# Gate pairs by seven half-width products, an input cut into blocks, and a second attention moved forward by a conv tile

## The chip, the cores and the metric

One core of a Trainium2 chip runs the whole program. The metric is the time of one execution on the device in microseconds (us); lower is better. The engines go by the profile's names: PE is TensorE (matmuls), PEld its weight loads, DVE is VectorE, ACT is ScalarE, POOL is GpSimd, SP is SyncE, which here issues all DMAs. All five run their own instruction streams in a fixed order and wait for one another by semaphores.

## What is computed

Two layers over a sequence of 512 positions with 1024 channels, batch 1, all in float32. Each layer:

```
h = rms_norm(x, norm_g[l])
p = h @ w_in[l]                          # 1024 -> 8776 columns, split among the mixers and the merge gates
y_a = short_conv_mixer(...)              # 512 wide, width-3 causal conv, gates, then @ w_out_conv (512 -> 1024)
y_b = sparse_attention_mixer(...)        # 8 heads of 64; an indexer picks 128 keys a query; then @ w_out_attn
y_c = pool_mixer(...)                    # causal means over 2, 4, 8, 16 positions; then @ w_out_pool
g = sigmoid(mgate.reshape(B, S, 3, D))   # three gates of 1024 columns each, from p
merged = g[:, :, 0] * y_a + g[:, :, 1] * y_b + g[:, :, 2] * y_c
x = x + merged @ w_o[l]
```

## The kernel before

Everything is held transposed: channels on the 128 partitions, the 512 positions along the free axis. The normalized input is 8 tiles of 128 x 512, and each weight column block of 128 is a chunk of 128 x 1024 (8 k-tiles side by side), streamed from HBM. To keep float32's precision with matmuls of type float32r, every operand is split into a high and a low part: ScalarE copies it to float32r (`hi`), VectorE subtracts that from the source (`lo`), and `mm3` (L393) forms hi*hi + hi*lo + lo*hi, three matmuls for each k-tile.

A projection (`project`, L456) is thus 8 k-tiles x 3 matmuls of 512 columns into one PSUM tile of tag `pj` (four of them). `take` and `prep` (L362 to L381) keep the weights three chunks ahead: a load of 512 KB, ScalarE's copy (L371), VectorE's subtraction (L372). `load_x` (L415) splits the input times `norm_g` into `xh`; the root-mean-square factor `rb` of each position comes later, as a multiplication when a projection leaves PSUM (`evac`, L383).

A layer runs, in program order: the indexer's projections and rotary embedding; four pool tiles, with the selection of keys (`select`, L556; long sequences of VectorE instructions); `merge` for branch C; q and k projections of heads 0 to 3 (`qk_quad`, L679, with norm, rotary embedding and DMAs that stack heads by partitions); v; attention of heads 0 to 3 among the gate projections of the attention (L773); four conv tiles of four projections each (L780), with the second `qk_quad` at tile 3 (L781) and the second `attention` behind them (L803); `merge` for branch A (gates "gA") and branch B ("gB"); and the output projection w_o (L826).

`merge` (L591) takes the 1024 gate columns in four pairs of 128-column tiles. For a pair: two projections of the input (2 x 24 matmuls), evacuated by `rb` and through a tanh (sigmoid(g) is written as (tanh(g/2) + 1)/2), then two output projections `py` of the mixer's 512 channels (2 x 12 matmuls), a product of gate and `py` on VectorE (L608), and a sum into `acc` on POOL (L610). With the last branch the sum is split into `mh`, `ml` for w_o.

The order of work is not that of the program. A planner (`Order`, L30 to L299) reads all instructions, gives each a cost (`cost`, L108) and a latency between engines (L37), plays them through list scheduling (`play`, L139) under the numbers of buffers of every tag, and fixes each engine's order by what came out best in PASSES tries (`arrange`, L247). On PE the priority is program order; what is later fills PE wherever what is earlier isn't ready.

SBUF tags that the change touches: `b` (tiles of 128 x 4 x 512, eight of them), `xhi`/`xlo` (one buffer for each k), `k` (one: the stacked keys of an attention), `ptr` (two: transposed scores), `score1` to `score3`, `h`, `z`, `a`, `w`.

Of the kernel before, what the change touches and what calls it, by code (L numbers as in the profile page):

```python
# [5 lines left out]
F32 = mybir.dt.float32  # L6
F32R = mybir.dt.float32r
# [5 lines left out]
PASSES = 4  # L13
# [16 lines left out]
class Order:  # L30
# [7 lines left out]
    TO_PE = {"PE": 0.003, "DVE": 0.255, "Activation": 0.27, "Pool": 0.2, "SP": 0.27}  # L38
# [37 lines left out]
    def read(self):  # L76
        ops, hist, memo = [], {}, {}
        for inst in self.tc.nc.cur_bb.bb.instructions[self.start:]:
# [6 lines left out]
            for aps, w in ((inst.ins, False), (inst.outs, True)):  # L85
                for a in aps:
                    if hasattr(a, "bass_ap"):
# [4 lines left out]
                        acc.append((w,) + memo[key])  # L92
            for w, name, (p0, p1), mask in acc:
                tiles.append(name)
                h = hist.setdefault(name, [])
                for j, wj, q0, q1, m in h:
                    if (w or wj) and p0 < q1 and q0 < p1 and (isinstance(m, dict) or isinstance(mask, dict) or m & mask):
                        deps.add(j)
# [9 lines left out]
    def cost(self, inst, kind):  # L108
# [14 lines left out]
        if kind == "InstMatmult":  # L123
            f32 = str(aps[0].dtype).endswith("float32")
            c = (0.0004167 * n + 0.003) * ((4 if n > 128 else 2) if f32 else 1)
# [6 lines left out]
        if engine == "Pool":  # L132
            return (0.1 if kind == "InstMemset" else 0.1 + 0.0022 * n), 0.0
        if kind in ("InstMax", "InstMatchReplace"):
            return 0.069 + 0.00104 * max(size(a) for a in aps), 0.0
# [167 lines left out]
def trunk(ctx, tc, xT, wst, vecs, cst, outT):  # L303
# [6 lines left out]
    bp = pool("bp", 8)  # L310
# [46 lines left out]

    wq = {}
# [3 lines left out]
    def prep(i):  # L362
        l, c = divmod(i, NCHUNK)
        raw = wp.tile([P, 1024], F32, tag="raw", name=nm("raw"), bufs=2)
        hi = wp.tile([P, 1024], F32R, tag="whi", name=nm("whi"), bufs=3)
        lo = wp.tile([P, 1024], F32R, tag="wlo", name=nm("wlo"), bufs=3)
        n = 1024 // (4 if i == 0 else 2 if i < 3 else 1)
        for j in range(0, 1024, n):
            p = slice(j, j + n)
            load(raw[:, p], wst[l, c, :, p])  # L370
            act.activation(hi[:, p], raw[:, p], AF.Copy)  # L371
            dve.tensor_tensor(out=lo[:, p], in0=raw[:, p], in1=hi[:, p].bitcast(F32), op=ALU.subtract)  # L372
        wq[i] = (hi, lo)

    def take():
        i = state["used"]
        state["used"] += 1
        while state["next"] <= min(i + LOOK - 1, DEPTH * NCHUNK - 1):
# [36 lines left out]
    def load_x(l, k, xt):  # L415

        g = vt[:, l, V_G + k:V_G + k + 1]
# [57 lines left out]
    for l in range(DEPTH):  # L475
# [115 lines left out]
        def merge(yh, yl, acc, first, last):  # L591
            for d2 in range(0, KT, 2):
                gs = []
                for _ in range(2):
# [6 lines left out]
                for e, g in enumerate(gs):  # L601
                    d = d2 + e
                    py = pj()
# [176 lines left out]
        for i in range(4):  # L780
            if i == 3:  # L781
                quad = qk_quad()
# [161 lines left out]
```

## Time and profile before

| | |
|---|---|
| median of 3 runs | 1079.21 us (1078.87 to 1079.73) |
| the profiled execution | 1078.84 us, of which the span of its instructions is 1077.1 us |
| PE busy | 1065.4 us (99%), 4842 matmuls |
| PEld busy | 878.4 us, 4842 loads |
| DVE busy | 799.2 us (74%), 1389 instructions |
| ACT busy | 465.5 us (43%) |
| POOL busy | 97.2 us (9%) |
| HBM read / written | 101.49 / 4.19 MB, 98 GB/s over the span |
| TensorE's granted clock | 1.00 in every stretch asked for below |

The trace is of one execution, with times in microseconds from the first instruction. The busy time of PE is a union of recorded matmuls, each of which overlaps the next, so the distance from one start to the next start says what a matmul costs in a row. A group of instructions is named by its line in the kernel, its engine, and what it writes and reads (`pj<-xhi,whi`), with buffer numbers left out; nearly all matmuls have line 388, that of the helper `mm`.

### The profile page before, as it was taken

The numbers are of one execution on the slowest core, as the hardware profiler recorded it, in microseconds if no ns is written. First come the engines' busy times: TensorE is split into PE (matmuls) and PEld (weight loads), VectorE is DVE, ScalarE is ACT, GpSimd is POOL, SyncE is SP. The second block draws the span as 40 slices with busy tenths as digits, with TensorE's granted clock in tenths as the row PEclk, the third lists the DMA queues.
The fourth block names the chain that finished last, engine by engine and source line by source line (L and its number), as shares of the span: only waits on it lengthen the run. The fifth ranks groups of instructions, "written<-read, shape, count | busy, mean of one in ns | idle before, by whom it ended". The sixth has DMA issues, their size and how long they took to land.

```text
span 1077.1 us, 13444 instructions
## 1 busy us (share of the span) xinstructions
PE 1065.4 (99%) x4842; PEld 878.4 (82%) x4842; DVE 799.2 (74%) x1389; ACT 465.5 (43%) x747; POOL 97.2 (9%) x76
## 2 busy tenths in 40 slices
PE   7999999999999999999999999999999999999998
PEld 6888888888888888888888888888888878888886
DVE  6889999997558865455559899999876598744442
ACT  6355233485233673233334542235852347623320
POOL 4000000000000011221210000000000001132210
PEclk9999999999999999999999999999999999999999
DMA  6542322452234522234535322225423245122352
GB/s 226 153 140 78 99 98 94 133 152 72 82 102 130 160 75 78 98 98 164 169 117 153 115 86 98 98 79 166 128 79 98 79 144 149 61 98 98 98 195 78
DMA packets 44402, 124.39 MB, mean 115 GB/s; under 512 B 6960, under 2 KB 7472, under 8 KB 44336
## 3 DMA queue, kind: packets, MB, share of 16 engines
q1 hardware_dynamic: 44336, 123.53, 36.4%
q8 instruction: 38, 0.62, 0.2%
q14 instruction: 28, 0.23, 0.1%
HBM read 101.49 MB, written 4.19 MB: 98 GB/s over the span
## 4 chain that ended last, share of the span: by engine, by line
PE 96%; DVE 1%; DMA 1%; issue 0%; ACT 0%; SPq 0%; DVEq 0%; ACTq 0%
PE pj L388 87%; PE sc L388 4%; PE pv L388 3%; PE pt L391 2%; DMA b<-in_x 0%; DVE wlo L372 0%; DMA k<-h 0%; DVE w L488 0%; SPq L355 0%; DVE h L401 0%; ACT whi L371 0%; DVE w L649 0%; ACT xhi L403 0%; DVE w L435 0%; DVE w L436 0%
## 5 line engine op out<-in xcount | busy, mean ns | idle before, releaser
L388 PE MATMUL pj<-xhi,whi 128*128 128x512 f32 x1040 | 373.1, 393 | 6.5 <-ACT whi L371 6.5
L388 PE MATMUL pj<-xlo,whi 128*128 128x512 f32 x1040 | 372.8, 393 | 0.0
L388 PE MATMUL pj<-xhi,wlo 128*128 128x512 f32 x1040 | 372.4, 393 | 0.0
L371 ACT ACTIVATE whi<-raw 128x1024 fp32r<-128x1024 f32 (+2 forms) x185 | 191.5, 1036 | 385.6 <-PE pj L388 358.9
L372 DVE TENSOR_TENSOR wlo<-raw,whi 128x1024 fp32r<-128x1024 f32 (+2 forms) x185 | 228.5, 1239 | 15.5 <-ACT whi L371 14.8
L388 PEld LDWEIGHTS pj<-xhi,whi 128*128 128x128 f32 x1040 | 195.0, 188 | 46.7 <-ACT whi L371 6.7
L388 PEld LDWEIGHTS pj<-xhi,wlo 128*128 128x128 f32 x1040 | 195.7, 188 | 39.4 <-DVE wlo L372 0.5
L388 PEld LDWEIGHTS pj<-xlo,whi 128*128 128x128 f32 x1040 | 195.5, 188 | 39.4
L388 PE MATMUL pj<-b,whi 128*128 128x512 f32 x640 | 210.7, 390 | 0.0
L385 DVE TENSOR_TENSOR w<-pj,ss 128x512 f32<-128x512 f32 x104 | 70.8, 684 | 93.3 <-PE pj L388 93.0
L388 PEld LDWEIGHTS pj<-b,whi 128*128 128x128 f32 x640 | 120.0, 188 | 24.2
L388 PE MATMUL pj<-b,wlo 128*128 128x512 f32 x320 | 118.2, 391 | 0.0
L610 POOL TENSOR_TENSOR b<-b,w 128x512 f32<-128x512 f32 x32 | 60.6, 1899 | 264.5 <-DVE w L608 264.4
L388 PEld LDWEIGHTS pj<-b,wlo 128*128 128x128 f32 x320 | 60.1, 188 | 12.3
L576 DVE MAX8 m<-score 128x8 f32<-128x256 f32 (+2 forms) x96 | 53.2, 557 | 1.7
L577 DVE MATCH_REPLACE8 score<-m,score 128x384 f32<-128x384 f32 (+2 forms) x96 | 52.0, 542 | 0.0
L742 DVE TENSOR_TENSOR pth<-pt,pth 128x128 fp32r<-128x128 f32 (+1 forms) x64 | 31.1, 486 | 18.7 <-PE pv L388 9.4
L819 DVE TENSOR_TENSOR w<-pj,w 128x512 f32<-128x512 f32 x16 | 11.0, 690 | 44.4 <-PE pj L388 42.8
L727 ACT ACTIVATE a<-a,mn 128x128 f32<-128x128 f32 (+1 forms) x64 | 35.6, 557 | 15.5 <-DVE mn L724 14.9
L665 POOL TENSOR_TENSOR w<-w,w 128x512 f32<-128x512 f32 x8 | 11.9, 1492 | 325.4 <-ACT w L664 325.4
L388 PE MATMUL pv<-pth,b 128*128 128x512 f32 (+3 forms) x128 | 39.9, 316 | 0.0
L741 ACT ACTIVATE pth<-pt 128x128 fp32r<-128x128 f32 (+1 forms) x64 | 27.6, 432 | 27.4 <-PE pt L391 20.1
(119 smaller groups left out, 999.7 us busy)
## 6 DMA issues: line engine op xcount, KB each, us to landing
raw<-in_w SPq DMA_DIRECT2D x177, 512.0 KB, 3.3
b<-h SPq DMA_DIRECT2D x128, 64.0 KB, 2.2
k<-h SPq DMA_DIRECT2D x64, 128.0 KB, 3.2
b<-in_x SPq DMA_DIRECT2D x8, 256.0 KB, 4.8
w<-in_x SPq DMA_DIRECT2D x8, 256.0 KB, 5.5
xs<-w SPq DMA_DIRECT2D x8, 256.0 KB, 2.3
w<-xs SPq DMA_DIRECT2D x8, 256.0 KB, 3.9
out_x<-w SPq DMA_DIRECT2D x8, 256.0 KB, 2.0
```

Source lines behind the costliest of these rows:

```text
L371: act.activation(hi[:, p], raw[:, p], AF.Copy)
L372: dve.tensor_tensor(out=lo[:, p], in0=raw[:, p], in1=hi[:, p].bitcast(F32), op=ALU.subtract)
L385: dve.tensor_tensor(out=out, in0=ps, in1=by, op=ALU.mult)
L388: pe.matmul(ps, lhs, rhs, start=start, stop=stop)
L391: pe.transpose(out, src, ident if n == P else ident[64:64 + n, 64:64 + n])
L576: dve.max(m8, score)
L577: dve.match_replace(score, m8, score, -3.0e38)
L610: gp.tensor_tensor(out=a, in0=a, in1=g, op=ALU.add)
L665: gp.tensor_tensor(out=s0, in0=s0, in1=s1, op=ALU.add)
L727: act.activation(pr[:, :w], pr[:, :w], AF.Exp, bias=mn, scale=-1.0, accum_out=zs)
L741: act.activation(dh, pst[:, :b + 1, :], AF.Copy)
L742: dve.tensor_tensor(out=dl, in0=pst[:, :b + 1, :], in1=dh.bitcast(F32), op=ALU.subtract)
```

## The change

Five of the eight gate pairs of branches A and B in each layer (the last pair of "gA", all four of "gB") are computed by Strassen's scheme. The 256 gate columns x 1024 channels of a pair are cut into 2 x 2 blocks (two column tiles by two halves of the channels, four k-tiles each), the input into 2 x 2 blocks (two halves of the channels by two halves of 256 positions). Instead of eight block products there are seven, on sums of blocks. `build` makes the input's blocks once a layer, behind the conv tiles: it loads x again, multiplies by `norm_g` and `rb`, and splits three blocks and four sums into tiles of the tags `b`, `k`, `ptr` and `score`. `prep` makes the sums of weights of each pair from two raw chunks (the layout in HBM has the same number of chunks). `blocks` does the seven products of 12 matmuls of 256 columns, and adds them up on VectorE. The signs are such that one gate's sum comes out negative, hence the `sign` at the tanh.

Besides: the second `qk_quad` goes from conv tile 3 to conv tile 1 and the second attention from behind the conv tiles to conv tile 3; `xh` moves into tiles of tag `b` (twelve instead of eight); `py` of the block pairs uses the PSUM tag `sc`; the planner's costs for matmuls, POOL and one VectorE instruction are changed, its latency from PE to PE becomes 0, PSUM accesses are widened to whole banks when it looks for dependences, and it makes six passes.

```diff
@@ constants, class Order
-PASSES = 4
+QUAD, ATT = 1, 3
+FIRST = 3
+PASSES = 6
-    TO_PE = {"PE": 0.003, "DVE": 0.255, "Activation": 0.27, "Pool": 0.2, "SP": 0.27}
+    TO_PE = {"PE": 0.0, "DVE": 0.255, "Activation": 0.27, "Pool": 0.2, "SP": 0.27}
+        def banks(mask):
+            bank = (1 << S) - 1
+            return (bank if mask & bank else 0) | (bank << S if mask >> S else 0)
...
-            c = (0.0004167 * n + 0.003) * ((4 if n > 128 else 2) if f32 else 1)
+            c = (0.000423 * n + 0.01) * ((4 if n > 128 else 2) if f32 else 1)
...
-            return (0.1 if kind == "InstMemset" else 0.1 + 0.0022 * n), 0.0
+            return (0.1 if kind == "InstMemset" else 0.1 + 0.003 * n), 0.0
...
-    bp = pool("bp", 8)
+    bp = pool("bp", 12)
@@ prep
+        if part == 1:
+            raw = big(F32)
+            c0, c1 = (raw[:, 2 * j:2 * j + 2].rearrange("p a b -> p (a b)") for j in range(2))
+            load(c0, wst[l, c])
+            load(c1, wst[l, c + 1])
+            state["raw"] = c0, c1
+            split(hi, lo, c0)
+            ah, al = (wk.tile([P, S], F32R, tag="a", name=nm("ua"), bufs=4) for _ in range(2))
+            split(ah, al, c1[:, S:])
+            wq[i] += (ah, al)
+            return
+        c0, c1 = state["raw"]
+        a22, a11, a21, a12 = c0[:, :S], c0[:, S:], c1[:, :S], c1[:, S:]
+        u = wk.tile([P, 2, S], F32, tag="h", name=nm("u"), bufs=2)
+        if part == 2:
+            dve.tensor_tensor(out=u[:, 0], in0=a21, in1=a22, op=ALU.add)
+            dve.tensor_tensor(out=u[:, 1], in0=u[:, 0], in1=a11, op=ALU.add)
+            state["s2"] = u[:, 1]
+        else:
+            dve.tensor_tensor(out=u[:, 0], in0=a21, in1=a11, op=ALU.add)
+            dve.tensor_tensor(out=u[:, 1], in0=state["s2"], in1=a12, op=ALU.add)
+        split(hi, lo, u.rearrange("p a b -> p (a b)"))
@@ load_x
-        hi = xp.tile([P, S], F32R, name=nm("xhi"), tag=f"xhi{k}")
-        lo = xp.tile([P, S], F32R, name=nm("xlo"), tag=f"xlo{k}")
-        split(hi, lo, xt, g)
-        xh[k] = (hi, lo)
+        if k % 4 == 0:
+            xh["b"] = big(), big()
+        xh[k] = tuple(b[:, k % 4] for b in xh["b"])
+        split(*xh[k], xt, vt[:, l, V_G + k:V_G + k + 1])
@@ new: build (the loop over k)
+            for k in range(4):
+                x = []
+                for j in range(2):
+                    xj = A() if j else wk.tile([P, S + 16], F32, tag="z", name=nm("z"), bufs=3)[:, :S]
+                    load(xj, xT[k + 4 * j] if l == 0 else xs[k + 4 * j])
+                    g = vt[:, l, V_G + k + 4 * j:V_G + k + 4 * j + 1]
+                    dve.scalar_tensor_tensor(xj, xj, g, rb, op0=ALU.mult, op1=ALU.mult)
+                    x += [xj[:, :q], xj[:, q:]]
+                x11, x12, x21, x22 = x
...
+                split(*t["11", k], x11)
...
+                split(*t["21", k], x21)
...
+                split(*t["22", k], x22)
+                uv = wk.tile([P, 2, S], F32, tag="h", name=nm("uv"), bufs=2)
+                u, v = uv[:, 0], uv[:, 1]
+                dve.tensor_tensor(out=u[:, :q], in0=x11, in1=x12, op=ALU.subtract)
+                dve.tensor_tensor(out=v[:, :q], in0=u[:, :q], in1=x22, op=ALU.add)
+                dve.tensor_tensor(out=u[:, q:], in0=x22, in1=x12, op=ALU.subtract)
+                dve.tensor_tensor(out=v[:, q:], in0=v[:, :q], in1=x21, op=ALU.subtract)
...
@@ new: product and blocks
+        def product(out, part, at, t, name):
+            hi, lo = part
+            for k in range(4):
+                c = slice(at + k * P, at + (k + 1) * P)
+                mm3(out, hi[:, c], lo[:, c], *t[name, k], k == 0, k == 3)
+
+        def blocks(t, a, b):
+            w1, w2, w3 = take(), take(), take()
+            w1, w4 = w1[:2], w1[2:]
...
+            p0, p1, p2, p3 = pj(), pj(), pj(), pj()
+            s, u = W(), W()
...
+            product(p0[:, h0], w1, S, t, "11")
+            act.activation(s[:, h0], p0[:, h0], AF.Copy)
+            product(p2[:, h1], w1, 0, t, "4")
+            product(p3[:, h1], w2, S, t, "2")
+            add(s[:, h1], s[:, h0], p3[:, h1], ALU.subtract)
+            product(p1[:, h0], w2, 0, t, "1")
+            product(p1[:, h1], w3, 0, t, "3")
+            add(pair(u), pair(p1), s[:, h1].unsqueeze(1).to_broadcast([P, 2, q]))
+            add(b[:, h1], p1[:, h0], u[:, h1])
+            add(b[:, h0], p2[:, h1], u[:, h1])
+            product(p2[:, h0], w3, S, t, "22")
+            add(a[:, h1], p2[:, h0], u[:, h0])
+            product(p3[:, h0], w4, 0, t, "21")
+            add(a[:, h0], p3[:, h0], s[:, h0])
@@ merge
+                t = d2 >= 2 * plain
+                if t:
+                    gs = [W(), W()]
+                    blocks(bt, *gs[::-1])
+                    for g, sign in zip(gs, (-1, 1)):
+                        act.activation(g, g, AF.Tanh, scale=0.5 * sign)
...
-                    py = pj()
+                    py = sc() if t else pj()
@@ the layer
-            if i == 3:
+            if i == QUAD:
                 quad = qk_quad()
+            if i == ATT:
+                attention(1, *quad)
...
-        attention(1, *quad)
-        merge(yh, yl, acc, False, None)
+        build()
+        merge(yh, yl, acc, False, None, FIRST)
...
-        merge(yh, yl, acc, False, (mh, ml))
+        merge(yh, yl, acc, False, (mh, ml), 0)
```

## Rows read from the trace of the kernel before

**Rows 1.** the page: busy time of the engines; tenths busy in 40 slices

```profile
PE 1065.4 (99%) x4842; PEld 878.4 (82%) x4842; DVE 799.2 (74%) x1389; ACT 465.5 (43%) x747; POOL 97.2 (9%) x76
...
PE   7999999999999999999999999999999999999998
...
DVE  6889999997558865455559899999876598744442
```

**Rows 2.** PE's waits: for whom, us in total, times, the longest

```profile
PE pj L388 <- ACT whi L371: 6.5, 1, 6.5
PE sc L388 <- DVE w L649: 0.6, 1, 0.6
```

**Rows 3.** PE's timeline from 207 us: start, length, line, tiles, shape, count

```profile
207.02 0.62 PE L388 MATMUL pj<-xhi,wlo 128*128 128x512 f32 x2
...
208.83 0.62 PE L388 MATMUL pj<-xhi,whi 128*128 128x512 f32 x2
```

**Rows 4.** PE's timeline in the index scores

```profile
74.47 0.28 PE L388 MATMUL sc<-b,b 128*128 128x256 f32 x1
74.58 0.40 PE L388 MATMUL pj<-xlo,whi 128*128 128x512 f32 x1
74.82 0.40 PE L388 MATMUL sc<-b,b 128*128 128x256 f32 x2
75.06 0.40 PE L388 MATMUL pj<-xhi,wlo 128*128 128x512 f32 x1
```

**Rows 5.** the weight loads' timeline there

```profile
74.94 0.19 PEld L388 LDWEIGHTS pj<-xhi,wlo 128*128 128x128 f32 x1
```

**Rows 6.** DVE's instructions by form: count, busy us, mean ns of one, idle before

```profile
L372 DVE TENSOR_TENSOR wlo<-raw,whi 128x1024 fp32r<-128x1024 f32 x177 | 219.2, 1242 | 15.2 <-ACT whi L371 14.6
...
L488 DVE SCALAR_TENSOR_TENSOR w<-w,vt,w 128x512 f32<-128x512 f32 x32 | 22.7, 745 | 0.0
...
L742 DVE TENSOR_TENSOR pth<-pt,pth 128x256 fp32r<-128x256 f32 x16 | 6.7, 417 | 0.1
...
L401 DVE TENSOR_TENSOR w<-w,w 128x512 fp32r<-128x512 f32 x8 | 5.5, 683 | 3.9 <-ACT w L400 3.7
```

**Rows 7.** DVE's timeline within a pair of branch B

```profile
459.58 2.36 DVE L372 TENSOR_TENSOR wlo<-raw,whi 128x1024 fp32r<-128x1024 f32 x2
...
467.53 2.61 DVE L404 SCALAR_TENSOR_TENSOR b<-b,b 128x512 fp32r<-128x512 f32 x2
```

**Rows 8.** four stretches of layer 0: busy us (instructions) of each engine, PEclk, DMA

```profile
271.00:328.00 57.00, 57.00 (x253) 47.20 (x252) 32.67 (x42) 17.66 (x21) 1.40 (x2) 1.00 0.29 93
328.00:361.00 33.00, 33.00 (x145) 26.52 (x143) 32.25 (x45) 12.04 (x16) 1.93 (x1) 1.00 0.49 148
361.00:410.00 49.00, 48.68 (x251) 40.42 (x251) 35.47 (x91) 36.65 (x85) 6.16 (x4) 1.00 0.33 94
410.00:492.00 82.00, 82.00 (x363) 67.88 (x362) 40.70 (x45) 25.86 (x32) 17.62 (x10) 1.00 0.30 96
```

**Rows 9.** tile k on PE from 328 us: ns min/median/max, first and last start

```profile
L388 PE MATMUL sc<-k,b x32: 220/334/483, 361.4 to 392.0; 128*128 128x128 f32 x8, 128*128 128x256 f32 x8, 128*128 128x384 f32 x8, 128*128 128x512 f32 x8
```

**Rows 10.** tile pth on PE from 328 us, the same columns

```profile
L388 PE MATMUL pv<-pth,b x32: 222/306/483, 373.6 to 409.6; 128*128 128x512 f32 x8, 128*128 128x384 f32 x8, 128*128 128x256 f32 x8, 128*128 128x128 f32 x8
```

**Rows 11.** tile z on DVE in the conv tiles of layer 0

```profile
L385 DVE TENSOR_TENSOR z<-pj,ss x4: 662/687/692, 241.4 to 339.0; 128x512 f32<-128x512 f32 x4
```

**Rows 12.** DMA issues: count, KB each, median us to landing

```profile
raw<-in_w SPq DMA_DIRECT2D x177, 512.0 KB, 3.3
```

**Rows 13.** the timeline of all engines about one wait of PE

```profile
604.14 0.39 PE L388 MATMUL sc<-h,wlo 128*128 128x512 f32 x1
604.57 0.75 DVE L649 SCALAR_TENSOR_TENSOR w<-sc,vt,w 128x512 f32<-128x512 f32 x1
...
605.38 0.39 PE L388 MATMUL sc<-b,b 128*128 128x256 f32 x1 [0.61 <-DVE w L649]
```

**Rows 14.** line 610 on POOL from 410 to 492 us

```profile
L610 POOL TENSOR_TENSOR b<-b,w x10: 1288/1780/2265, 416.1 to 482.8; 128x512 f32<-128x512 f32 x10
```

More of the change, by code (lines that the diff above doesn't have):

```diff
@@ L355, in load @@
         nc.sync.dma_start(dst, src)
+    units = []
+    for l in range(DEPTH):
+        kinds = _kinds()
+        for c, kind in enumerate(kinds):
+            if kind == "plain":
+                units.append((l, c, 0))
+            elif kind == "blocks":
+                units += [(l, c, 1), (l, c, 2), (l, c, 3)]
     wq = {}
@@ L362, in prep @@
     def prep(i):
-        l, c = divmod(i, NCHUNK)
-        raw = wp.tile([P, 1024], F32, tag="raw", name=nm("raw"), bufs=2)
+        l, c, part = units[i]
         hi = wp.tile([P, 1024], F32R, tag="whi", name=nm("whi"), bufs=3)
         lo = wp.tile([P, 1024], F32R, tag="wlo", name=nm("wlo"), bufs=3)
[L367 to L372, printed above, removed]
-        wq[i] = (hi, lo)
+        wq[i] = (hi, lo)
+        if part == 0:
+            raw = wp.tile([P, 1024], F32, tag="raw", name=nm("raw"), bufs=2)
+            n = 1024 // (4 if i == 0 else 2 if i < 3 else 1)
+            for j in range(0, 1024, n):
+                p = slice(j, j + n)
+                load(raw[:, p], wst[l, c, :, p])
+                split(hi[:, p], lo[:, p], raw[:, p])
+            return
[9 more added lines that the diff above has]
+            wq[i] += (ah, al)
+            return
+        c0, c1 = state["raw"]
[9 more added lines that the diff above has]
+        split(hi, lo, u.rearrange("p a b -> p (a b)"))
     def take():
@@ L377, in take @@
         state["used"] += 1
-        while state["next"] <= min(i + LOOK - 1, DEPTH * NCHUNK - 1):
+        while state["next"] <= min(i + LOOK - 1, len(units) - 1):
             prep(state["next"])
@@ L592, in merge @@
+        def merge(yh, yl, acc, first, last, plain=4):
             for d2 in range(0, KT, 2):
                 gs = []
-                for _ in range(2):
+                t = d2 >= 2 * plain
[4 more added lines that the diff above has]
+                        act.activation(g, g, AF.Tanh, scale=0.5 * sign)
+                for _ in range(0 if t else 2):
                     ps = project()
@@ L856, in _columns @@
     for i in range(4):
-        if i == 3:
+        if i == QUAD:
             t += ab(q, 1) + ab(k, 1)
@@ L861, in _columns, with _kinds, _blocked @@
     return t, v, mg
+def _kinds():
+    kinds = []
+    for t in _columns()[0]:
+        if isinstance(t, str) and t[0] == "g":
+            for d in range(4):
+                kinds += (["blocks", "second"] if _blocked(t, d) else ["plain"] * 2) + ["plain"]
+        else:
+            kinds.append("plain")
+    return kinds + ["plain"] * KT
+def _blocked(gate, d):
+    return gate == "gB" or gate == "gA" and d >= FIRST
 def _layout(x, norm_g, w_in, conv_w, w_out_conv, q_norm_g, k_norm_g, w_out_attn, pool_w, pool_scale, w_out_pool, w_o):
@@ L867, in _layout, with pair @@
     wst = np.zeros((DEPTH, NCHUNK, P, 1024), np.float32)
+    def pair(dst, w, a, b):
+        h = KT // 2
+        for j, x in enumerate((w[:, h:, b], w[:, :h, a], w[:, :h, b], w[:, h:, a])):
+            dst[j // 2, :, (j % 2) * S:(j % 2 + 1) * S] = x.reshape(P, S)
     outs = {"gA": (0, w_out_conv), "gB": (1, w_out_attn), "gC": (2, w_out_pool)}
```

59 lines of the change are left out of this document (48 added, 11 removed).

## The prediction

> **What bounds the kernel now.** I read the page's busy table and its 40 slices first: TensorE (PE) is busy 1065.4 of 1077.1 us and every slice but the first and the last shows 9, while VectorE (DVE) stands at 9 only in two stretches and at 4 to 7 in the merges [rows 1]. The second view asks what PE itself waited for: 6.5 us for the first weights, and then 0.6 us as the longest item [rows 2]. So the time is the sum of PE's pitches, and an edit pays if it takes columns from PE without making PE wait. The price of a matmul is its pitch, start to start, not its recorded duration, which overlaps the next one's. At 512 columns eight matmuls start in 208.83 - 207.02 = 1.81 us, 0.2265 us each [rows 3].
>
> **Seven products for eight.** A gate pair now takes two projections of 8 k-tiles with 3 matmuls each: 48 matmuls of 512 columns, 48 x 0.2265 = 10.87 us. After the change it takes 7 products of 4 k-tiles with 3 matmuls: 84 matmuls of 256 columns. The pitch at 256 columns is in the index scores: one such matmul from 74.47 to the next start at 74.58, two from 74.82 to 75.06, 0.35 us for three, 0.1175 each [rows 4]. The weights of the matmul at 75.06 begin to load at 74.94, with the 256-wide one ahead of it [rows 5], so a load for every matmul fits into that pitch. 84 x 0.1175 = 9.87 us. A pair saves 1.0 us; five pairs in each of two layers, **-10.0 us**. The second matmul of a pair and the output projection (24 matmuls, 512 wide) stay as they are; that it writes another PSUM tag moves no column.
>
> **What DVE gains in work.** Its durations by form overlap the next instruction by 0.08 us (two of 1024 take 2.36 us end to end, one about 1.22 [rows 6, 7]). So an instruction on 1024 columns occupies 1.14 us, on 512 0.60, on 256 0.34, and one with a per-partition scalar on 512 0.67 [rows 6].
> Per pair in the gB merge, before: three weight splits 3.42, two evacuations 1.20, two gate products 1.20, two splits of the sum 1.30: 7.1 us. After: splits of two-column-block submatrices 3 x 1.14 + 0.60, four weight sums 2.40, the output weights' split 1.14, the sums of products 0.60 + 5 x 0.34 = 2.30, gate products 1.20, splits of the sum 1.30: 12.4 us, **+5.3 us** on DVE beside 15.3 us of PE (9.87 + 24 x 0.2265).
> The input's blocks, once per layer: for each of four k, two scalings 1.34, three splits 1.02, four sums 1.36, one split of 1024 or its pieces 1.14 to 1.36: about 4.9, **19.5 us** per layer. Together 19.5 + 5 x 5.3 = 46 us a layer, 92 in all: DVE goes from 799 to about 890 us. ScalarE gains about 1.5 splits of 1024 a pair and the x splits, far from its limit.
> Is there room? From 361 to 492 us of layer 0 DVE is busy 35.5 + 40.7 of 131 us and idle 55 [rows 8]; layer 1 is taken as alike. The work fits, with 9 us to spare. None of it lies on PE's path as long as each piece comes in time; the rest of the sum is where it doesn't.
>
> **The blocks before their first product.** The blocks' tiles are those of attention's second half: its keys, its transposed scores, the values. They come free when its scores (361.4 to 392.0 us) and values (to 409.6) are done [rows 9, 10]. The last gA pair and four gB pairs are 360 matmuls, 81.5 us, so they fill 410 to 492 [rows 8]: in the old order the blocks would have no time at all. That is what QUAD and ATT are for. The quarter's q and k projections go ahead of conv tiles 1 and 2, and the attention stands ahead of conv tile 3, whose 96 matmuls (21.8 us) now lie behind it. So attention ends at least 22 us ahead of the first block product. It ends 28 us or more ahead if its scores start when conv tile 2's matmuls are issued: the last conv tile's first evacuation is at 339.0, so its 24 matmuls (5.4 us) began by 333.6 [rows 11], while the scores waited for their keys until 361.4 [rows 9]. Those keys were late because DVE was busy 32.3 of 33 us from 328 to 361; from 271 to 328, where the rotary work now falls, it is busy 32.7 of 57 [rows 8]. In 22 to 28 us the plain merge pairs (5.8 us of DVE by the list above, in 16.3) leave DVE idle for 64%, 14 to 18 us, for 19.5 us of blocks, all of which the first two products need; two k's loads, scalings and sums (5.4 us) need no tile of attention's. So the first product is 0 to 5.5 us late per layer. I take 1.5, near the good end, because DVE's idle time from 271 to 328 speaks for the early start. **+3 us** (0 to +11). What the move pushes past: on SP's queue eight x loads of 256 KB a layer stand among the weight loads of 512 KB (3.3 us to land [rows 12]); an x load that waits for its tile holds the weights behind it. On POOL nothing is added. Covered while the weights are two units ahead; otherwise it is part of the same lateness.
> The pair's raw weights now take a big tile, and the count of those live (x 4, sums 2, y 2, attention output 1, blocks 3) is twelve of twelve until the third gA pair's second projection is half done: 36 matmuls or 8.2 us before the first product, against 3.3 for the load [rows 12], 1.2 for DVE's split and about as much for the ScalarE copy ahead of it. It just fits; nothing added.
>
> **Inside a pair.** Three DVE sums follow the fifth product, the last of them reading one half of a PSUM tile whose other half is the sixth product's target. The changed planner widens every PSUM access to its bank, so the sixth product stands behind them. A DVE instruction starts 0.04 us after the recorded end of the matmul that it reads (604.14 + 0.39, then 604.57), and a matmul 0.06 after the DVE instruction that frees its tile (604.57 + 0.75, then 605.38) [rows 13]. A 256-wide matmul is recorded with 0.28 [rows 4], of which PE would lose all but its pitch: 0.16 + 0.04 + 0.60 + 0.34 + 0.42 + 0.06 = 1.6 us. The planner may fill it with the pair's 24 output matmuls (5.4 us), which need neither the sums nor the gate. Zero to 1.6 a pair, 0 to 16 in all. I take 0.1 a pair, **+1**, since PE shows next to no wait now in stages with just such chains [rows 2].
> The Trainium skill (PSUM — Partial Sum Buffer, PSUM bank collisions raise a hardware error) says that two engines may not touch one bank in one quadrant at once even in different columns; no row here shows it. By that page alone the wait is a must and the price 1.6 us wherever nothing fills it.
>
> **The planner's new figures.** Matmul costs rise by 10 ns to 0.2266 at 512, which is what the trace has [rows 3]; the orders of the whole kernel are made anew with six passes. PE's waits leave at most 2 us to win outside the first weights [rows 2], and a new order may lose as much: 0, from -2 to +2. "A sum goes on in its PSUM tile" is, as far as the diff shows, only this: the planner's PE-to-PE latency becomes 0. No product is accumulated on another.
>
> **Sum.** Against the profiled execution's 1078.84 us (span 1077.1 and 1.7 around it; the median of the runs is 1079.21): 1078.84 - 10.0 + 3 + 1 = **1072.8 us**.
>
> **The rivals.** (a) **The blocks come late**: only 22 us remain, or the loads don't keep up; 5.5 us a layer, 1068.8 + 11 + 1 = 1080.8. For it: the blocks (19.5), two plain pairs (11.6) and five new pairs (62) are 93 us of DVE in the 22 + 80 us from attention's end to the last gB pair, over 90%. Against: the idle DVE from 271 to 328. It eats the gain from 5 us a layer on.
> (b) **The bank wait is not filled** (the slower side): ten times 1.6 at the sixth product of each pair, 1068.8 + 3 + 16 = 1087.8. From 0.7 us a pair on nothing is won. For it: engines run in fixed orders, and a DVE queue that is behind turns a planned filler into a wait. Against: 5.4 us of filler in the same pair.
> (c) **DVE becomes the bound of the gB merge.** GpSimd's sums take 1.29 us alone and up to 2.27 [rows 14], and two splits beside them take 2.61 us [rows 7] instead of 1.3, some 0.6 more a piece. Two a pair make 12.4 + 1.2 = 13.6 of 15.3: not the bound, and 12.4 + 2 x 1.29 = 15.0 is still not. The Trainium skill (SBUF — State Buffer, Who interferes with whom) says that a DVE instruction with two SBUF inputs and a GpSimd instruction that reads SBUF share one read port and exclude each other; the rows agree. With more late answers it gives 1 us a pair: 1068.8 + 3 + 10 = 1081.8.
> (d) **256 columns don't hold their pitch** over 84 matmuls in a row; these rows have two. At 0.125 the saving is 0.4 a pair: 1078.84 - 4 + 4 = 1078.8. (e) The new order alone costs or gains over 2 us.
>
> **How the numbers follow.** Forecast (1067 to 1076.5) 0.66; (a) with its softer forms 0.11; (b) 0.08; (c) 0.05; (d) 0.06; (e) 0.04. A measurement of this kernel can tell about 0.2%, 2.2 us, from no change: faster means under 1077.0, slower over 1081.4. Nearly all of the forecast and a third of the others is faster: 0.76. Of (b) nearly all, of (a), (c) and (e) somewhat under half is slower: 0.14. Same 0.10. The range leaves out some 0.08 below (no wait at all and 2 us from the new order) and 0.1 above ((b) and the hard form of (a)): 1067 to 1083.
>
> **What would show it.** 840 matmuls of 256 columns on the blocks' tiles at a pitch of 0.117, and 480 fewer of 512; PE's wait list with under 3 us a layer for the blocks' splits and under 0.3 us a pair at the sixth product; second-attention values ending 22 us or more ahead of the first block product; DVE near 890 us busy. The prediction is wrong if the pitch lies above 0.125, if PE waits for DVE over 5 us a layer, or if PE's idle time appears in a stage that the change doesn't touch.

## The result, and the profile after

The change makes the kernel slower: 1086.12 us median of 4 runs (1085.43 to 1086.72) against 1079.04 (1078.71 to 1079.73) for the kernel before beside it, ratio 1.0065 [1.0047, 1.0082]. The forecast was 1072.8 with a range up to 1083.0. The profiled execution took 1086.72 us, with a span of 1084.9.

The page of the changed kernel: busy time of the engines, and tenths busy in 40 slices.

```profile
PE 1063.6 (98%) x5202; PEld 884.2 (82%) x5202; DVE 892.1 (82%) x1575; ACT 496.2 (46%) x815; POOL 91.1 (8%) x76
...
PE   7999999999999999999999999999999999999998
...
DVE  6999999987687997886549999999767889798842
```

Against [rows 1], PE has 5202 matmuls for 4842 (840 narrow ones more, 480 wide ones fewer), DVE 93 us more work, and PE is idle for 1084.9 - 1063.6 = 21.3 us where it was idle for 11.7. The columns saved are worth 8.7 us at the pitch measured below (the forecast had 10.0), yet PE's busy time falls by 1.8 only. That is no contradiction: busy time is a union of recorded lengths. A 256-column matmul is recorded with 0.28 us and followed after 0.12, one of 512 columns with 0.39 and followed after 0.23, so the last one ahead of a stall adds 0.16 us of busy time that moves no column. A run below shows how much this can be: in another order of the kernel before (the planner's new figures alone), the same 4842 matmuls at the same granted clock keep PE busy for 4.6 us more.

```profile
PE 1070.0 (99%) x4842; PEld 874.9 (81%) x4842; DVE 804.8 (74%) x1389; ACT 459.8 (42%) x747; POOL 84.0 (8%) x76
```

PE's waits in the changed kernel: for whom, us in total, times, the longest.

```profile
PE pj L434 <- ACT whi L446: 5.8, 2, 5.2
PE pj L434 <- DVE w L704: 3.8, 6, 1.0
PE pj L434 <- DVE wlo L447: 2.4, 4, 1.1
PE sc L434 <- ACT w L446: 1.8, 2, 0.9
PE pt L437 <- DVE w L574: 1.1, 2, 0.6
PE sc L434 <- ACT h L446: 0.9, 1, 0.9
```

In [rows 2] there was one item over 0.6 us, the first weights. Now there are several. The second line is that of the change itself: L704 is `add`, the sums of the seven products. The fifth and sixth lie in the first 70 us of a layer, in the indexer and the first pool tile, which the change leaves alone; the fourth lies in the second q and k projections, which it only moves.

PE's timeline in the changed kernel: in each layer the first pair's late weights, then the three waits on the sums.

```profile
425.30 0.39 PE L434 MATMUL pj<-th,wlo 128*128 128x256 f32 x1 [1.10 <-DVE wlo L447]
425.52 0.28 PE L434 MATMUL pj<-th,whi 128*128 128x256 f32 x1
...
429.32 0.28 PE L434 MATMUL pj<-th,wlo 128*128 128x256 f32 x1
...
446.10 1.70 PE L434 MATMUL pj<-b,ua 128*128 128x256 f32 x12 [1.00 <-DVE w L704]
...
477.57 1.69 PE L434 MATMUL pj<-b,ua 128*128 128x256 f32 x12 [0.25 <-DVE w L704]
...
481.30 0.51 PE L434 MATMUL pj<-b,whi 128*128 128x256 f32 x2 [0.66 <-DVE w L704]
...
960.29 0.38 PE L434 MATMUL pj<-th,wlo 128*128 128x256 f32 x1 [0.55 <-DVE wlo L447]
...
981.08 1.69 PE L434 MATMUL pj<-b,ua 128*128 128x256 f32 x12 [0.99 <-DVE w L704]
...
1012.55 1.69 PE L434 MATMUL pj<-b,ua 128*128 128x256 f32 x12 [0.25 <-DVE w L704]
...
1016.28 0.50 PE L434 MATMUL pj<-b,whi 128*128 128x256 f32 x2 [0.65 <-DVE w L704]
```

`pj<-b,ua` is the seventh product (block "21", weights `ua`), which the program issues last and the plan has moved forward as filler; `pj<-b,whi` is the sixth ("22"). What holds the seventh at 446.10 is on DVE's timeline at that place; POOL's one instruction there stands in the second fence. The lines from 473 us on belong to the wait at 477.57.

```profile
442.20 0.68 DVE L417 TENSOR_TENSOR u<-b 128x512 f32<-128x512 f32 x1
442.80 1.77 DVE L418 TENSOR_TENSOR u<-u,b 128x512 f32<-128x512 f32 x1
444.50 1.21 DVE L447 TENSOR_TENSOR wlo<-raw,whi 128x1024 fp32r<-128x1024 f32 x1
445.63 0.41 DVE L704 TENSOR_TENSOR w<-w,pj 128x256 f32<-128x256 f32 x1
...
474.27 1.78 DVE L450 SCALAR_TENSOR_TENSOR b<-b,b 128x512 fp32r<-128x512 f32 x1
...
477.44 0.68 DVE L418 TENSOR_TENSOR u<-u,b 128x512 f32<-128x512 f32 x1
```

```profile
442.36 1.67 POOL L745 TENSOR_TENSOR b<-b,w 128x512 f32<-128x512 f32 x1 [3.09 <-DVE w L743]
...
473.90 1.61 POOL L745 TENSOR_TENSOR b<-b,w 128x512 f32<-128x512 f32 x1 [3.15 <-DVE w L743]
```

The sum at 445.63 (called at L709 of the changed kernel) reads one half of `p3`, whose other half is the seventh product's target. It could run from the third product's last matmul on, at 441.97, but it stands behind two weight sums, one of which takes 1.77 us beside POOL where the same line takes 0.68 at 477.44, and behind a split of later weights. So the seventh product starts 446.10 - 444.81 = 1.29 us after the matmul ahead of it, where the pitch is 0.12.

The long instruction is no single case. In the block pairs of both layers (410 to 512 and 940 to 1045 us) ten DVE instructions on 512 columns take 1.45 to 1.79 us where their like take 0.68. Each runs beside one of POOL's sums, and each ends about 0.55 us behind that sum's end (442.80 + 1.77 against 442.36 + 1.67). Together they cost DVE 9.7 us. The four waits of the seventh product and the two for late weights all come within 4 us behind one of 1.77 to 1.79 us.

### The profile page after: what moved, and what is told of

The parts are those of the page before. It is cut to its first block, busy times and chain, and to the rows that moved or that the text cites. A ratio compares the mean times of both kernels' runs of the same rounds, so it can differ in the third digit from the quotient of the medians.

```text
span 1084.9 us, 14478 instructions
## 1 busy us (share of the span) xinstructions
PE 1063.6 (98%) x5202; PEld 884.2 (82%) x5202; DVE 892.1 (82%) x1575; ACT 496.2 (46%) x815; POOL 91.1 (8%) x76
## 4 chain that ended last, share of the span: by engine, by line
PE 78%; DVE 10%; issue 4%; ACT 3%; DMA 3%; SPq 1%; POOL 1%; DVEq 0%; ACTq 0%; POOLq 0%
PE pj L434 66%; PE sc L434 7%; DVE wlo L447 3%; PE pv L434 3%; PE pt L437 2%; DMA b<-h 2%; DMA raw<-in_w 1%; DVE b L450 1%; ACT whi L446 1%; DVE w L704 1%; SPq L366 1%; DVE u L412 1%; POOL w L800 1%; ACT a L862 0%; DVE u L418 0%
## 5 line engine op out<-in xcount | busy, mean ns | idle before, releaser
L434 PE MATMUL pj<-b,whi 128*128 128x512 f32 (+1 forms) x2400 | 736.8, 385 | 7.6 <-ACT whi L446 5.8
L434 PEld LDWEIGHTS pj<-b,whi 128*128 128x128 f32 x2400 | 445.0, 189 | 94.4 <-ACT whi L446 6.3
L434 PE MATMUL pj<-b,wlo 128*128 128x512 f32 (+1 forms) x1200 | 462.1, 385 | 0.8 <-DVE wlo L447 0.7
L434 PEld LDWEIGHTS pj<-b,wlo 128*128 128x128 f32 x1200 | 226.4, 189 | 43.2 <-DVE wlo L447 2.0
L622 DVE MATCH_REPLACE8 score<-m,score 128x256 f32<-128x256 f32 (+2 forms) x96 | 52.0, 543 | 0.0
L434 PE MATMUL sc<-b,whi 128*128 128x512 f32 x160 | 50.0, 392 | 0.0
L434 PE MATMUL pj<-th,wlo 128*128 128x256 f32 x160 | 45.0, 282 | 1.7 <-DVE wlo L447 1.7
L434 PE MATMUL pj<-th,whi 128*128 128x256 f32 x160 | 45.0, 281 | 0.0
L865 ACT ACTIVATE a<-a,rz 128x128 f32<-128x128 f32 (+1 forms) x64 | 34.2, 555 | 3.8 <-DVE rz L864 3.5
L434 PE MATMUL pj<-tl,whi 128*128 128x256 f32 x120 | 33.9, 282 | 0.0
```

The lines of the kernel that those rows point to most:

```text
L434: pe.matmul(ps, lhs, rhs, start=start, stop=stop)
L622: dve.match_replace(score, m8, score, -3.0e38)
L865: act.activation(pr[:, :w], pr[:, :w], AF.Copy, scale=rz)
```

## The experiments

All times are medians; the kernel before took 1078.5 to 1079.0 us beside them. Every edit that touches the planner's figures or the instructions makes it arrange the whole kernel anew, in most cases to another order. Where the text names figures that a cut does not show, the run has them too.

### Which part of the diff costs

The change with the planner's figures of before (matmul, POOL, match-replace, PE latency, four passes); its bank-wide view of PSUM stays:

```diff
-PASSES = 6
+PASSES = 4
...
-    TO_PE = {"PE": 0.0, ...
+    TO_PE = {"PE": 0.003, ...
...
-            c = (0.000423 * n + 0.01) * ...
+            c = (0.0004167 * n + 0.003) * ...
...
```

> The change, with the planner's old costs, latency and four passes (its view of whole PSUM banks stays). PE waits 16.5 us more in the changed kernel than before, by PE's lag behind its own matmuls: 8.0 in the ten block pairs, 8.5 elsewhere (3.4 up to 200 us of layer 0, 1.1 in the same stage of layer 1, 3.4 at the conv tiles of both, 0.6 at the second attentions). Theory P: what lies elsewhere comes from the new figures; then some 4 to 8 us come back, 1078 to 1082. Rival M or X: it comes from the moved attention or from the input in big tiles; then the time stays at 1084 to 1088.

Measured 1079.03 us, ratio 0.9999 [0.9989, 1.0008]. With the old figures the change costs nothing and gains nothing; with the new ones it takes 7.1 us more. Now the new figures without the change:

```diff
+PASSES = 6
...
+    TO_PE = {"PE": 0.0, ...
...
+            c = (0.000423 * n + 0.01) * ...
...
+            return (0.1 if kind == "InstMemset" else 0.1 + 0.003 * n), 0.0
+            return 0.069 + 0.00104 * n + 0.076 * (kind == "InstMatchReplace"), 0.0
```

> The kernel before with the planner's new costs, latency and six passes alone. Theory P: 4 to 8 us slower than before, 1083 to 1087, with new waits of PE in the first 80 us. Rivals M and X: within 1 us of before, 1078 to 1080.

Measured 1084.96 us, 1.0052 [1.0035, 1.0069]: a loss of 6.0 us, nearly that of the change, without a single product changed. The other two parts alone, first the move, then the big tiles:

```diff
+            if i == 1:
+                quad = qk_quad()
             if i == 3:
-                quad = qk_quad()
+                attention(1, *quad)
...
-        attention(1, *quad)
...
```

> The kernel before with the second q and k projections at conv tile 1 and the second attention at conv tile 3 alone. Theory M: the 1.7 us a layer at the conv tiles appear, 1082 to 1083. Rival P: within 1 us of before, 1078 to 1080.

Measured 1078.07 us, 0.9991 [0.9981, 1.0000]: the move costs nothing.

```diff
-    bp = pool("bp", 8)
+    bp = pool("bp", 12)
...
+        if k % 4 == 0:
+            xh["b"] = big(), big()
+        xh[k] = tuple(b[:, k % 4] for b in xh["b"])
...
```

> The kernel before with the input's splits in big tiles of tag b (twelve of them) alone. Theory X: the 2 to 3 us of waits in the first 40 us appear, 1081 to 1082. Rival P: within 1 us of before, 1078 to 1080.

Measured 1078.90 us, ratio 0.9999 [0.9990, 1.0008]: no cost either, and PE's matmuls come in just the order of before. The planner's bank-wide view of PSUM was not run alone; it is in the first experiment, which lost nothing.

### Which of the figures

The change with the matmul cost and PE latency of before, the rest of its figures new:

```diff
-    TO_PE = {"PE": 0.0, ...
+    TO_PE = {"PE": 0.003, ...
...
-            c = (0.000423 * n + 0.01) * ...
+            c = (0.0004167 * n + 0.003) * ...
```

> The change with only the planner's matmul cost and its latency behind PE as before (a matmul of 512 columns 10 ns too cheap); the other new figures and the six passes stay. Theory: the matmul cost, which is right now, took from the plan a margin that a PE planned too fast had given it; then 5 to 8 us come back, 1078 to 1081. Rival: the other figures or the six passes did it; then 1084 to 1088.

Measured 1086.48 us (1083.14 to 1090.40), 1.0074 [1.0048, 1.0100]. No gain over the change, so the loss is not the matmul figure's alone. The same cut on the kernel before, the matmul figure and latency alone, then the others with the passes alone:

```diff
-    TO_PE = {"PE": 0.003, ...
+    TO_PE = {"PE": 0.0, ...
...
-            c = (0.0004167 * n + 0.003) * ...
+            c = (0.000423 * n + 0.01) * ...
```

> The kernel before with the planner's new matmul cost and PE latency alone, four passes. All new figures together cost 6.0 us (1085.0). Theory: a planner whose PE is 4.6% too fast leaves DVE that much margin, and the right figure takes it away; then this alone gives 1083 to 1087. Rival: the other figures or the two more passes do it; then 1078 to 1080.

```diff
-PASSES = 4
+PASSES = 6
...
-            return (0.1 if kind == "InstMemset" else 0.1 + 0.0022 * n), 0.0
+            return (0.1 if kind == "InstMemset" else 0.1 + 0.003 * n), 0.0
...
+            return 0.069 + 0.00104 * n + 0.076 * (kind == "InstMatchReplace"), 0.0
```

> The kernel before with the planner's new GpSimd and match-replace costs and six passes, the matmul cost as before. Theory of the matmul figure: 1078 to 1080. Rival, these figures or passes: 1082 to 1086. Third case, any new plan loses a few us that no figure explains: then both this and the matmul figure alone are slower than before.

Measured 1093.04 us, 1.0133 [1.0116, 1.0150], and 1082.09, 1.0030 [1.0018, 1.0042]. The parts, 14.0 and 3.1, do not add up to the 6.0 of both together. Costs that do not add up can hardly be costs of the figures; they pointed to the orders themselves.

### Is it the figure, or any new order?

The test is a figure that means nothing: the matmul cost of the kernel before times 1.002 and times 0.998, 0.4 ns on a 512-column matmul.

```diff
-            c = (0.0004167 * n + 0.003) * ...
+            c = 1.002 * (0.0004167 * n + 0.003) * ...
```

> The kernel before with the planner's matmul cost multiplied by 1.002 and nothing else. Theory S (each new order is a draw, and the kernel before had a good one): the time moves by several us although the figure hardly does, 1081 to 1088. Theory M (what the larger matmul figure takes away is planned slack of the other engines against PE): a twenty-fifth of 14 us, so 1079 +- 1.

> The kernel before with the planner's matmul cost multiplied by 0.998. Theory S: 1081 to 1088. Theory M: 1079 +- 1.

Measured 1088.71 us, 1.0097 [1.0082, 1.0112], and 1085.20, 1.0060 [1.0045, 1.0075]. Theory S (each new order is a draw) holds, though the first time lies 0.7 us above its stated range, and theory M (the figure takes away slack) has no answer to it: 0.2% on one figure costs 10.2 us in one direction and 6.7 in the other. The first 166 matmuls of the first of them come as in the kernel before; of all 4842 places, 3168 then hold a matmul of another name or shape. PE's waits in that kernel:

```profile
PE pj L388 <- ACT whi L371: 6.4, 1, 6.4
PE pj L388 <- DVE z L385: 3.4, 1, 3.4
PE sc L388 <- ACT w L400: 1.5, 2, 1.1
PE sc L388 <- ACT h L400: 0.6, 1, 0.6
```

The second line is one wait, of a matmul that starts at 588.14, in the indexer's stage of layer 1, where the kernel before has 0.6 us from 560 to 640. The matmul, and DVE's timeline ahead of it:

```profile
588.14 0.50 PE L388 MATMUL pj<-xhi,whi 128*128 128x512 f32 x1 [3.42 <-DVE z L385]
...
584.31 0.67 DVE L486 TENSOR_TENSOR w<-pj,ct 128x512 f32<-128x512 f32 x1
584.91 0.67 DVE L531 TENSOR_TENSOR w<-w,w 32x512 f32<-32x512 f32 x1
585.65 1.23 DVE L372 TENSOR_TENSOR wlo<-raw,whi 128x1024 fp32r<-128x1024 f32 x1
586.80 0.68 DVE L489 TENSOR_TENSOR w<-w,w 128x512 f32<-128x512 f32 x1
587.40 0.68 DVE L385 TENSOR_TENSOR z<-pj,ss 128x512 f32<-128x512 f32 x1
```

The evacuation that would free PE's PSUM tile stands last in a row of DVE instructions without a gap. It is the same kind of place as the seventh product's above: a fixed order in which DVE does something else first. The rest of the loss is in waits of 1.1 us and less, and in stalls too short for the list.

```diff
-            c = (0.0004167 * n + 0.003) * ...
+            c = (0.00042 * n + 0.0065) * ...
```

> The kernel before with a matmul cost half-way between the old figure (0.2163 us at 512 columns) and the new one (0.2266): 0.2215. Theory S: anything from 1078 to 1093, no order to it. Theory M: between the two, 1083 to 1088.

Measured 1089.14 us, 1.0104 [1.0087, 1.0120]: 10.6 us, hardly more than the 0.2% cost, so up to there the loss does not grow with the figure. It lies above theory M's range.

```diff
+    TO_PE = {"PE": 0.0, ...
...
+        M = 1.046
...
+            c = (0.000423 * n + 0.01) * ...
...
+            return M * (0.093 - 0.042 * psum + 0.000833 * n + 0.093 * extra), 0.0
...
+        return M * (0.069 + 0.00104 * n * (0.5 if fast else 1) + 0.061 * extra), 0.0
```

> The kernel before with the new matmul figure and PE latency, and the costs of ScalarE, GpSimd and VectorE multiplied by 1.046, the factor by which the matmul figure rose at 512 columns. Theory M: the slack of the other engines against PE is as in the kernel before, so most of the 14.0 us come back, 1079 to 1082. Theory S: another draw, so it comes out anywhere from 1079 to 1093, and only a time over 1085 speaks against M.

Measured 1082.62 us, 1.0039 [1.0024, 1.0054]. It is 10.4 us better than the matmul figure alone, close to what theory M asks (its range ended at 1082), but it lies inside the scatter of theory S too. That M has some part is not excluded; it is not needed.

The times for the work of the kernel before, in eight new orders: 1078.1 (the move), 1082.1, 1082.6, 1085.0, 1085.2, 1088.7, 1089.1 and 1093.0. Their mean is 1085.5, 6.5 above the kernel before, and their standard deviation 4.7. So the kernel before runs in a better order than seven of the eight. Whether the planner's own time for its orders would have told the good from the bad no run shows.

### The bank wait

The change with old figures (the first experiment), and the sixth and seventh product in PSUM tiles of their own:

```diff
+            p4, p5 = pv(), pt().rearrange("p a b -> p (a b)")
-            product(p2[:, h0], w3, S, t, "22")
-            add(a[:, h1], p2[:, h0], u[:, h0])
-            product(p3[:, h0], w4, 0, t, "21")
-            add(a[:, h0], p3[:, h0], s[:, h0])
+            product(p4[:, h0], w3, S, t, "22")
+            add(a[:, h1], p4[:, h0], u[:, h0])
+            product(p5[:, h0], w4, 0, t, "21")
+            add(a[:, h0], p5[:, h0], s[:, h0])
```

> The change with the planner's old figures (1079.0 us), and the last two products of a pair in PSUM tiles of their own (tags pv and pt), so that no product waits for a sum that reads the other half of its tile. PE's lag grows by 7.2 us in the block pairs of the two layers together. Bank theory: most of it goes, 1073 to 1076, and no wait of PE on the sums' line is left. Rival, DVE is late and PE would wait for the next thing: 1077.5 to 1079.5, with the same lag ended by other lines.

Measured **1073.61 us** (1072.37 to 1074.04), 0.9951 [0.9936, 0.9966]: faster than both kernels, and 5.4 us faster than with shared tiles. The same edit in the change as it stands, with the new figures:

> The change itself, new figures and all, with the last two products of a pair in PSUM tiles of their own. With the old figures these tiles were worth 5.4 us (1079.0 to 1073.6). Bank theory: about as much here, 1080 to 1083, and PE's waits on the sums' line (3.8 us in six) go. Rival, the plan's luck: no gain, or waits of other lines in their place, 1085 to 1090.

Measured 1079.13 us, 1.0000 [0.9990, 1.0009], 7.0 us faster than the change. Both are new orders as well, so two medians alone would say little. The trace carries it: windows over the block pairs of both layers, columns as in [rows 8], first of the change, then of the change with own tiles, whose list of waits has none for the sums.

```profile
410.00:492.00 82.00, 78.99 (x525) 72.08 (x524) 68.22 (x91) 36.58 (x50) 15.78 (x10) 1.00 0.26 92
...
940.00:1040.00 100.00, 97.47 (x624) 88.25 (x625) 79.54 (x106) 43.24 (x59) 23.13 (x15) 1.00 0.32 113
```

```profile
410.00:492.00 82.00, 81.22 (x551) 75.27 (x550) 69.47 (x94) 38.09 (x51) 15.83 (x10) 1.00 0.27 97
...
940.00:1040.00 100.00, 100.00 (x640) 91.15 (x639) 77.22 (x104) 42.52 (x57) 20.51 (x14) 1.00 0.33 119
```

PE's idle time falls from 3.0 + 2.5 to 0.8 + 0.0 us, by 4.8. Of that 3.8 us are the six waits listed for the sums; for the rest, the 1.7 us of waits for late weights go and one wait of 0.8 comes. The record ahead of each of the six hides 0.16 us more, so the sums' waits cost some 3.8 + 1.0 = 4.8 us. In the old figures' pair of kernels the same windows go from 2.1 + 2.2 to 0.5 + 0.0. The rest of the two differences is put down to the draw of the order. The kernel of 1073.6 us has ten DVE instructions of 1.67 to 1.79 us beside POOL in these stretches too, and PE next to no idle time: with own tiles the late DVE does not reach PE.

The 1073.6 us version with a matmul planned at 0.0004 us a column, to give the other engines still more room in the plan:

```diff
-            c = (0.0004167 * n + 0.003) * ...
+            c = (0.0004 * n + 0.003) * ...
```

> As the run with own banks, with a matmul planned another 4% too fast (0.0004 us a column). Margin theory: more of the waits go than by own banks alone, 1072 to 1076. Rival: the planner has no use for it or crowds other work; the same as own banks alone or slower.

Measured 1083.32 us, 1.0042 [1.0027, 1.0057]: 9.7 us worse, with single waits of 4.2 and 3.2 us outside the block pairs, each followed by a stretch at the lower granted clock (last section). More planned room is not better here; this is one more draw.

### GpSimd beside DVE

The change with old figures and without GpSimd's sums in the block pairs (the kernel leaves out the sum over branches there, and the splits read the gate product):

```diff
-                    if not first:
+                    if not first and not t:
                         gp.tensor_tensor(out=a, in0=a, in1=g, op=ALU.add)
...
-                        split(..., a, 0.5)
+                        split(..., g if t else a, 0.5)
```

> The change with the planner's old figures, and without GpSimd's sums in the block pairs (the sum over branches is left out there, and the splits read the gate product instead). Port theory: the DVE instructions of 512 that last 1.8 us beside a GpSimd sum fall to 0.7, DVE comes in time, and 3 to 6 us of the 7.2 go: 1073 to 1076. Rival: GpSimd isn't what makes DVE late, 1077 to 1079.5.

Measured 1087.56 us, 1.0079 [1.0063, 1.0096], slower although work is gone: PE waits 8.5 us in one piece ahead of the block pairs of layer 1 for an evacuation on DVE. Neither of the two expectations came true: it is a new order with an accident of its own, and its time tells nothing of what GpSimd costs. What it costs DVE is in the changed kernel's trace, 9.7 us in ten instructions (above); what that costs PE when the tiles are shared no run isolates.

### Was the move needed?

The 1073.6 us version with q and k projections at conv tile 3 and the attention behind the conv tiles, as in the kernel before:

```diff
-QUAD, ATT = 1, 3
+QUAD, ATT = 3, 4
+        if ATT == 4:
+            attention(1, *quad)
         build()
```

> Own tiles and old figures (1073.6 us), but the second q and k projections at conv tile 3 and the second attention behind the conv tiles as before. By the prediction's step the input's blocks then have no time between the attention's end and their first product: PE waits some 13 to 20 us in each layer ahead of the first block product, 1100 to 1113. Rival: the planner fills it with the rest, and the move was worth little: 1074 to 1080.

Measured 1112.24 us, 1.0308 [1.0293, 1.0323], 38.6 us more. PE's timeline where the blocks begin:

```profile
427.96 0.58 PE L433 MATMUL pj<-b,whi 128*128 128x256 f32 x1 [10.15 <-ACT whi L445]
428.34 0.42 PE L433 MATMUL pj<-th,whi 128*128 128x256 f32 x1
428.56 0.42 PE L433 MATMUL pj<-b,whi 128*128 128x256 f32 x1
428.77 0.42 PE L433 MATMUL pj<-tl,whi 128*128 128x256 f32 x1
```

The last matmul of the values starts at 414.8, and the first product starts at 427.96, behind a wait of 10.2 us; layer 1 has one of 11.0. Both were expected (1100 to 1113 us), and 38.6 us is well outside any scatter of orders seen here.

## Why the prediction was wrong, point by point

The working from 1072.8 to 1086.1, each term by the run that comes nearest to isolating it; the last two rows are differences between orders, with the scatter that these have:

| step | forecast | measured |
|---|---|---|
| seven products for eight | -10.0 | -8.7 |
| blocks before their first product | +3 | about 2: two waits for weights, 1.7, and 0.16 ahead of each |
| bank wait inside a pair | +1 | 5.4 by run, 4.8 by the six waits |
| the planner's new figures | 0, from -2 to +2 | +7.1 in the change, +6.0 alone |

The first, third and fourth miss by 1.3, 4.4 and 7.1 us, the second came out about 1 better: 11.8 of the 13.3 by which the time missed. The rest is below the scatter of orders (next). The measured time lies near the 1087.8 of rival (b), but by chance: of (b)'s 16 us under a third was there, most of it at the seventh product.

**The planner's new figures: the step that failed.** The prediction argued that PE's waits "leave at most 2 us to win" and that "a new order may lose as much". The first half was read from [rows 2]; the second came from no row. A kernel with next to no wait can hardly gain by a new order but can lose a lot, so the term is lopsided. That is what the runs show in its place: eight new orders of the same work ran from 0.9 below the kernel before to 14.0 above it. Rival (e) had the mechanism, at 0.04, with no sign and no size but "over 2 us". That PE now waits where nothing was edited is what the last sentence of the prediction named as proof against it.

**The bank wait: right mechanism, wrong size and place.** Rival (b) had it at the sixth product in every pair. The trace has six waits in ten pairs, two at the sixth (0.66 and 0.65 us) and four at the seventh (1.00, 0.25, 0.99, 0.25). The prediction counted the pair's own work as filler; the planner used the seventh product as filler, which stands behind the same kind of wait on `p3`'s bank, and DVE was later than its plan: the planner's cost for the sum that took 1.77 us is 0.60. "PE shows next to no wait now in stages with just such chains" was the weak argument: in the gate pairs of the kernel before each product fills a whole PSUM tile, so no matmul there stands behind the reader of another product's half. That the chip asks for this wait no run shows; the planner asks for it. The 16 us of rival (b) were too much, the 1 us of the forecast too little.

**256 columns.** 32 pitches from 425.52 to 429.32 us in the changed kernel are 3.80 us, 0.119 each, against 0.1175 from two in [rows 4]. 84 x 0.119 = 10.0 us where 48 wide ones took 10.87, so a pair saves 0.87 us. Rival (d) with 0.125 is out, the forecast a little high.

**The blocks in time, and the move.** Right, and the move is needed, as its undoing shows. The values of the second attention end at 377.5 us, 43 us ahead of the first block product at 420.95, better than the 22 to 28 of the forecast, and that product waits for nothing. What is late is a pair's weights: 1.1 us at 425.30 and 0.55 at 960.29, for the splits of the weight sums. Ahead of both DVE loses 1.1 us in the split of `ua` beside POOL's sum, and in layer 0 it first waits 0.47 us for a load. The loads of raw blocks land in 5.5 us, where [rows 12] gave 3.3. The second attention's values, the first block product, DVE's wait, and the loads:

```profile
L434 PE MATMUL pv<-pth,b x32: 220/311/483, 345.8 to 377.5; 128*128 128x512 f32 x8, 128*128 128x384 f32 x8, 128*128 128x256 f32 x8, 128*128 128x128 f32 x8
...
420.95 0.40 PE L434 MATMUL pj<-b,whi 128*128 128x256 f32 x2
...
419.32 0.69 DVE L412 TENSOR_TENSOR u<-b 128x512 f32<-128x512 f32 x1 [0.47 <-DMA b<-in_w]
...
raw<-in_w SPq DMA_DIRECT2D x157, 512.0 KB, 3.5
b<-in_w SPq DMA_DIRECT2D x20, 512.0 KB, 5.5
```

"It just fits; nothing added" was thus a little too kind.

**DVE.** Forecast about 890 us, measured 892.1. Rival (c) does not show: in the block pairs' windows DVE is busy 68 of 82 and 80 of 100 us. But ten DVE instructions beside GpSimd took 0.8 to 1.1 us longer (0.68 to between 1.45 and 1.79), where the rival reckoned with 0.6 a piece from [rows 7]; DVE does not become the bound by them, it comes late where PE waits. The Trainium skill (SBUF — State Buffer, Who interferes with whom) says that a DVE instruction with two SBUF inputs and a GpSimd instruction that reads SBUF contend for a shared port pair, and that this pair is an exclusive lock. The rows agree: each of the ten ends about 0.55 us behind GpSimd's sum, about as if it had started there.

**What the seven products are worth.** By the best order of each, the work of before 1078.1, the change 1079.0, the change with own tiles 1073.6. By the mean of the orders tried, 1085.5 (eight), 1083.9 (three) and 1078.7 (three); with a scatter of 4.7 us the means of three are good to some 3 us. With shared tiles no gain is shown; with the tiles parted the scheme gains 4.5 us by the best orders and some 7, give or take 3, by the means.

Left open: why the figures of before give a good order, by chance or because they leave room; and how much of the sums' waits would go if GpSimd stayed away from DVE instead of the tiles being parted.

## What to carry to other kernels

Where a planner fixes the order of a kernel that is nearly free of waits, any edit that reaches the planner is a new draw: price it by measuring the old work under a few meaningless changes of a cost (here 0.2%, for 7 to 10 us), put that scatter into the range, on the slow side, and search orders again before judging an edit. Where the plan takes a PSUM tile as one, a scheme that packs two products into its halves ties its matmuls to the reader of the other half, so give them tiles of their own where there are any. For transfers of work off PE, look where DVE's fixed queue puts the instruction that PE waits for, not at DVE's busy share, and at which of the instructions ahead of it run beside GpSimd.

## What the runs showed of the hardware

In the kernel with the move undone, TensorE's granted clock fell to its lower level (0.50, the 1.2 GHz one) during the 10.2 us wait, and was still there for the first matmuls behind it. Windows of that kernel, columns as in [rows 8]:

```profile
405.00:417.00 12.00, 12.00 (x61) 9.82 (x60) 5.92 (x10) 3.41 (x7) 1.24 (x1) 1.00 0.21 67
417.00:428.00 11.00, 0.85 (x5) 0.39 (x3) 10.75 (x20) 7.26 (x16) 1.87 (x3) 0.66 0.49 166
428.00:432.00 4.00, 3.71 (x16) 3.42 (x17) 4.00 (x7) 2.01 (x3) 0.00 (x0) 0.50 0.50 198
...
436.00:445.00 9.00, 7.41 (x51) 6.57 (x52) 9.00 (x17) 4.06 (x5) 0.00 (x0) 1.00 0.32 116
```

From 428.34 to 428.77 two pitches of 256 columns take 0.43 us, 0.215 each for 0.119, so this wait cost more than itself.

Shorter waits did it too. With the matmul figure alone a wait of 2.3 us ends at 716.69, and from 718 us on matmuls of 512 columns start 0.43 us apart for 0.23:

```profile
718.00:719.00 1.00, 1.00 (x3) 0.76 (x3) 0.99 (x3) 0.23 (x1) 0.00 (x0) 0.50 0.00 0
```

```profile
718.19 0.63 PE L388 MATMUL pj<-xlo,whi 128*128 128x512 f32 x1
718.62 0.63 PE L388 MATMUL pj<-xhi,wlo 128*128 128x512 f32 x1
```

It is at 1.00 again from 722 us. The planner's matmul at 0.0004 us a column had 0.50 behind its wait of 4.2 us (221 to 226 us) and about as low behind that of 3.2 (0.53 from 766 to 769). The wait of 3.4 us in the run with 1.002 was followed by 1.00. So some of the new orders lost a little by the clock besides their waits; the changed kernel did not (1.00 throughout).

And a stall of PE loses about 0.16 us more than the list of waits says, behind a matmul of 256 columns as of 512, since the record of that matmul runs on into it.
